# Delta rule: merges of the second and third batch of triangles moved into the attention's loop

## The chip, the cores and the metric

The kernel runs on one core of one Trainium2 chip. The core has TensorE (PE), VectorE (DVE), ScalarE (ACT), GpSimd (POOL) and SyncE (SP, which here only issues transfers), an on-chip memory of 128 partitions (SBUF), a small accumulator memory of 8 banks for matmul results (PSUM), and 16 DMA engines to and from DRAM. Each engine runs its own queue in order. The metric is device time of one launch in microseconds (us), the median of several runs.

## The reference

Two layers of a diffusion backbone work on 256 context tokens and 512 latent tokens of width 1024. A layer normalises and modulates its input, projects it once with `w_in`, and runs two groups of heads beside each other: softmax attention, and a gated delta rule in both directions. Their outputs are joined by `w_out`, and a mixture of experts follows. The delta rule is the part that matters here. It is computed in chunks of 64 tokens, and each chunk needs the inverse of a unit lower triangle:

```
lower = where(strict, einsum("bhnid,bhnjd->bhnij", kb, kc) * decay, 0)
tmat  = triangular_solve(lower + eye, eye, lower, unit_diagonal)   # 64 x 64, per head, chunk and direction
u, w  = tmat @ (vc * bc), tmat @ (kb * exp(gcum))

def step(state, xs):                     # 12 chunks, one after the other
    v_new = u_i - w_i @ state
    o_i   = qd_i @ state + a_i @ v_new
    state = state * exp(gl_i) + kd_i^T @ v_new
```

In the last layer only the latent tokens' output is needed.

## The kernel before

**Stages of a layer.** The input is normalised and projected (line 236 holds nearly all of these matmuls); within the projections the delta rule's triangles are prepared. Then comes a loop in which the attention, the 12 steps of the delta rule and the modulation vectors for later stages are interleaved. The output projection, the routing and the experts follow.

**Triangles.** The 12 chunks lie in six token tiles of two chunks. `PAIRS` makes three batches of them: tiles 0 and 1, tiles 2 and 5, tiles 3 and 4. Step s of the loop takes chunk s forwards and one chunk backwards, so steps 0 to 3 need batch 0, steps 4 and 5 batch 1, steps 6 and 7 batch 2, and so on. A 64 x 64 triangle is inverted in two halves. `delta_intra` (called by `intra_batch`) makes the triangles; it keeps the off-diagonal 32 x 32 blocks in SBUF tiles `uo` (line 799) and writes the diagonal blocks to DRAM (`db`). `delta_subst` loads these (`sB`), inverts them by 31 steps of two DVE instructions each (lines 821 and 822), one after the other, and writes the result to DRAM (`dy`). `delta_merge` loads the inverted blocks in another layout (`yl`, line 834, four transfers), transposes them on DVE (line 835), makes two masked copies for each direction on ACT (`xm`, line 840), multiplies by the off-diagonal blocks in two groups of 128 small matmuls (lines 848 and 852) with an eviction between them (line 849), adds the product on DVE (line 856), and stores the full inverse to DRAM (`xad`, line 857). `xm` has one buffer, so the copies for the second direction reuse it after the first direction's store has landed. The two products stand in one PSUM tile of two banks (`psS`), of which there is only one; the attention's scores (line 601) use the same.

**Order before the loop.** `ORDER` lists, for each layer, the projections and the delta rule's pieces in program order: `c` is a convolved projection, `n` a plain one, `i` is `intra_batch`, `s` is `delta_subst`, `m` is `delta_merge`, `x` the query products. All three merges stand near the end, `m2` last.

**The loop.** `kv_stacks` loads keys and values once projections are done (their tiles take over the place of the projections' inputs) and splits the keys into two parts, `ka` and `kb` (lines 569 to 575). `attn_queries` loads and splits queries (`ql`, lines 583 to 591). `attn_slots` runs the attention in units of one head and 128 queries, `ada_steps` the modulation: four weight loads of 1 MB and matmuls for a chunk of 1024, an accumulator `ac` (lines 264 and 266) and a store of it (line 280). `step_load` fetches a step's `lk`, `lx` and `lq` (lines 867 to 873). `PAT` interleaves the three by letters: `d` is the step, `f` the attention, `a` the modulation.

**What sets the order of work.** Nothing is pinned in these stages: `pin` acts only inside the experts. A planner goes through all instructions with its own estimate of durations, and takes among those that are ready the earliest in program order. So `ORDER` and `PAT` are priorities, and the result is one fixed order for each engine and each queue. A tile with all its buffers in use makes its next writer wait for the last reader.

Of the kernel before, what the change touches and what calls it, by code (L numbers as in the profile page):

```python
# [13 lines left out]
F32 = mybir.dt.float32  # L14
# [3 lines left out]
AF = mybir.ActivationFunctionType  # L18
# [23 lines left out]
def const_table():  # L42
# [4 lines left out]
    def put(name, a):  # L47
# [56 lines left out]
UO = 6  # L104
# [18 lines left out]
ORDER = ("c4 c5 c6 c7 S i0 s0 i1 s1 i2 s2 c0 c1 c2 c3 Q n256 n0 x n512 m0 m1 c8 c10 c11 c9 n2304 m2",  # L123
         "c4 c5 c6 c7 S c0 i0 s0 i1 s1 c9 i2 s2 c1 c2 c3 Q n256 n0 x n512 m0 m1 c8 c10 n2304 c11 m2")
# [17 lines left out]
class Model:  # L142
# [125 lines left out]
    def ada_steps(self, i, ch, pool, q):  # L268

        nc = self.nc  # L270
        eng = getattr(nc, q)
        acc = pool.tile([P, UNIT], F32, tag="ac", bufs=2, name="ac")
        ab = pool.tile([P, UNIT], F32, tag="ab", bufs=1, name="ab")
        eng.dma_start(ab, self.t["ada_b"][i, ch * D:(ch + 1) * D].rearrange("(g o j) -> g o j", g=4, o=1).to_broadcast([4, 32, UNIT]))
        for n in range(4):
            self.ada_part(i, ch, n, acc, lambda w, g: w[:, g * UNIT:(g + 1) * UNIT], pool, 2, q)
            if n < 3:
                yield
        nc.vector.tensor_tensor(acc, acc, ab, op=OP.add)
        eng.dma_start(self.md[i][ch], acc)  # L280
        yield
# [296 lines left out]
    def attn_queries(self, qd, pr, q0, nq, pool):  # L578

        nc, pin = self.nc, self.pin  # L580
        n = nq * P
        x = pool.tile([P, 4, P], F32, tag="ql", bufs=2, name="ql")
        self.q("att").dma_start(x[:, :nq], qd[:, q0:q0 + nq, pr * P:(pr + 1) * P])
        ps = self.psA("qt")
        for q in range(nq):
            pin(nc.tensor.transpose(ps[:, q * P:(q + 1) * P], x[:, q, :], self.ident))
        qs = pool.tile([P, 2, 512], F32R, tag="qs", bufs=2, name="qs")
        for e in range(2):
            o, r = 64 * e, 64 * (1 - e)
            pin(nc.scalar.activation(qs[o:o + 64, e, :n], ps[o:o + 64, :n], AF.Copy))  # L590
            pin(nc.vector.tensor_tensor(qs[r:r + 64, e, :n], ps[o:o + 64, :n], qs[o:o + 64, e, :n], op=OP.subtract))
        return qs
# [232 lines left out]
    def delta_merge(self, tts, dy, us, xad, pool):  # L825


        nc = self.nc
# [6 lines left out]
        nc.vector.transpose(yt, yl)  # L835
        xb, xt = (yt[:, 0], yl[:, 1]), (yl[:, 0], yt[:, 1])
        x = [pool.tile([P, 2, NH, HD], F32, tag="xm", bufs=1, name="xm") for d in range(2)]
        for d in range(2):
            for q in range(2):
                nc.scalar.activation(x[d][:, :, :, 32 * q:32 * q + 32], xb[d], AF.Copy, scale=self.C["quad"][:, q:q + 1])  # L840
        g = pool.tile([P, 512], F32, tag="mg", bufs=1, name="mg")
        ps = self.psS("mg")
        pa, pb = ps[:, :512], ps[:, 512:]
        place = [(d, 32 * (2 * c2 + d), 32 * (2 * c2 + 1 - d)) for d in range(2) for c2 in range(2)]
        blocks = [(t, h, slice((t * NH + h) * 32, (t * NH + h + 1) * 32)) for t in range(2) for h in range(NH)]
        for t, h, c in blocks:
            for d, ra, rb in place:
                nc.tensor.matmul(pa[rb:rb + 32, c], us[tts[t]][ra:ra + 32, h, :], xt[d][ra:ra + 32, t, h, :], start=True, stop=True, tile_position=(ra, rb))
        nc.scalar.activation(g, pa, AF.Copy, scale=-1.0)
        for t, h, c in blocks:  # L850
            for d, ra, rb in place:
                nc.tensor.matmul(pb[ra:ra + 32, c], g[rb:rb + 32, c], xb[d][rb:rb + 32, t, h, :], start=True, stop=True, tile_position=(rb, ra))
        a, b = tts
        for d in range(2):
            y = x[d][:, :, :, 32 - 32 * d:64 - 32 * d]
            nc.vector.scalar_tensor_tensor(y, pb.rearrange("p (t h i) -> p t h i", t=2, h=NH), self.C["quad"][:, d:d + 1], y, op0=OP.mult, op1=OP.add)
            self.q("ix").dma_start(xad[a:b + 1:b - a, d, :, 0].rearrange("t p f -> p t f"), x[d].rearrange("p t h i -> p t (h i)"))

    def step_load(self, s, vk, xad, qkd, need, pool):
# [9 lines left out]
        if need:  # L869
            a = pool.tile([P, 512], F32, tag="lq", bufs=2, name="lq")  # L870
            for d in range(2):
                self.q("step").dma_start(a[rows[d]], qkd[tl[d], rows[d]])
            nc.gpsimd.tensor_tensor(x[:, 1], x[:, 1], a, op=OP.mult)
# [7 lines left out]
    def delta_step(self, s, S, kx, dT, sc, o, seen, need, pool):  # L881
# [22 lines left out]
        if s > 0:  # L904
# [5 lines left out]
            t = pool.tile([P, 512], F32, tag="yt2", bufs=1, name="yt2")  # L910
# [85 lines left out]
    def intra_batch(self, b, us, dT, sc, xad, db, pool):  # L996
# [3 lines left out]
        for d in range(2):  # L1000
            for j, tt in enumerate(PAIRS[b]):
                n = 4 * (2 * d + j)
                self.delta_intra(tt, d, kk[j], sc, us[tt], xad, db[:, n:n + 4], pool)

# [497 lines left out]
    def layer(self, i, xsrc, rows, done, xstack, mod):  # L1502
# [12 lines left out]
        dy = [dr("dy%d_" % b, [NH, 16, 32, 32]) for b in range(3)]  # L1515
        qd, gd, atd = dr("qd", [P, NT, 768]), dr("gd", [P, NT, 512]), dr("atd", [P, 4, NT * P])
# [6 lines left out]
        with self.pool("hp", B) as hp:  # L1523
            with self.pool("pj", B) as wp:
# [47 lines left out]
                with self.pool("pp", B) as pool, self.pool("q1", A) as p1:  # L1572
# [7 lines left out]
                    for op in ORDER[i].split():  # L1580
# [10 lines left out]
                        elif kind == "i":  # L1591
                            self.intra_batch(int(arg), us, dT, sc, xad, db[int(arg)], p1)
                        elif kind == "s":
                            self.delta_subst(int(arg), db[int(arg)], dy[int(arg)], p1)
                        elif kind == "m":
                            self.delta_merge(PAIRS[int(arg)], dy[int(arg)], us, xad, p1)
# [8 lines left out]
        with self.pool("at", B) as pool:  # L1605
# [9 lines left out]
            with self.pool("q2", A) as p2:  # L1615
# [4 lines left out]
                for s in range(12):  # L1620
                    nkx = load(s + 1)
                    step = self.delta_step(s, S, kx, dT, sc, o, seen, need(D0[s] // 2), p2)
                    for c in PAT[i][s % 3]:
# [145 lines left out]
```

## Time and profile before

| | us |
|---|---|
| median of 3 runs | 2127.5 |
| lowest and highest | 2121.08 and 2129.52 |
| profiled execution | 2123.24 |
| its span | 2121.4 |

| engine | busy us | share of the span |
|---|---|---|
| PE | 1758.6 | 83% |
| DVE | 1272.5 | 60% |
| ACT | 882.0 | 42% |
| POOL | 839.4 | 40% |

The profile is one execution, recorded on the chip. Times are counted from its start. Busy shares are means over stages with different limits, so they are read by stretch. "PEclk" or "granted clock" is the share of full speed that TensorE got: 1.00 is 2.4 GHz and 0.50 is 1.2 GHz. The DMA share is the mean busy share of the 16 DMA engines. PEld is TensorE's loading of weights, which overlaps its matmuls. An `x` before a number is a count of instructions, and L835 is line 835. A row's square bracket holds the idle time of that engine just before it, and what ended it.

### The profile page before, as it was taken

To read this page: it belongs to the slowest core of one execution; us is meant where nothing else is said; L and a number is where in the kernel's file an instruction comes from. 1 tells how busy PE (TensorE), PEld (TensorE's weight loads), DVE (VectorE), ACT (ScalarE), POOL (GpSimd) and SP (SyncE) were. 2 spreads that over 40 slices of the span, in tenths; PEclk is the share of its full clock that TensorE was granted. 3 is DMA by queue.
4 is the path that set the end of the run, shared out by engine and by line. 5 is a ranking of instruction groups with operands and counts; after the bars stand their busy time and mean duration, and the time that the engine had idled before them with its cause. 6 is when DMAs were issued, how large, how long until landed. Compare 5 with 4: busy or idle time off the path is not lost. (4 is left out here: it accounts for less than half of the span.)

```text
span 2121.4 us, 34943 instructions
## 1 busy us (share of the span) xinstructions
PE 1758.6 (83%) x13579; PEld 1287.2 (61%) x13579; DVE 1272.5 (60%) x2350; ACT 882.0 (42%) x1513; POOL 839.4 (40%) x915
## 2 busy tenths in 40 slices
PE   6998785678887869999996987844897769999995
PEld 4886775456666745565555876733576555566553
DVE  3468995467672445655555579984677453444443
ACT  3454333446561124444444544423565223444442
POOL 4455663253254323324225467640334632233221
PEclk9998897779997989999997998976999779999997
DMA  8223445986627398889854323365972668887872
GB/s 279 72 70 90 117 137 144 260 250 204 195 56 171 103 359 315 328 319 324 327 180 122 92 73 110 93 182 148 311 204 71 177 266 311 328 312 303 313 262 85
DMA packets 227684, 427.76 MB, mean 202 GB/s; under 512 B 83721, under 2 KB 157181, under 8 KB 202940
## 3 DMA queue, kind: packets, MB, share of 16 engines
q1 hardware_dynamic: 171547, 329.09, 46.1%
q0 software_dynamic: 33536, 72.59, 12.1%
q10 hardware_dynamic: 22432, 23.81, 3.3%
q8 instruction: 109, 1.79, 0.4%
q14 instruction: 60, 0.48, 0.1%
HBM read 386.82 MB, written 84.67 MB: 222 GB/s over the span
## 5 line engine op out<-in xcount | busy, mean ns | idle before, releaser
L1351 PE MATMUL pab<-w,xt 128*128 128x512 f32 x1024 | 465.0, 597 | 0.5 <-ACT xt L1345 0.5
L1351 PEld LDWEIGHTS pab<-w,xt 128*128 128x128 f32 x1024 | 189.3, 192 | 191.2 <-issue 186.3
L1405 POOL DMA_INDIRECT yd<-ey,idx x64 | 118.8, 1856 | 469.8 <-DMA yd<-ey,idx 196.1
L1372 DVE TENSOR_TENSOR gl<-gt,gh 128x256 fp32r<-128x256 f32 x64 | 27.2, 425 | 276.9 <-ACT gh L1371 265.2
L1330 DVE TENSOR_TENSOR w2l<-w,w2h 128x2048 fp32r<-128x2048 f32 x64 | 147.3, 2301 | 43.5 <-ACT w2h L1329 40.8
L1371 ACT ACTIVATE gh<-gt 128x256 fp32r<-128x256 f32 x64 | 24.6, 385 | 349.1 <-PE gt L1367 349.1
L486 POOL TENSOR_TENSOR wlo<-wraw,whi 128x1024 fp32r<-128x1024 f32 (+1 forms) x44 | 111.1, 2530 | 83.5 <-ACT whi L485 83.5
L236 PE MATMUL pn<-whi,hh 128*128 128x256 f32 (+1 forms) x432 | 134.5, 314 | 8.7 <-ACT gev L1541 4.7
L236 PE MATMUL pn<-wlo,hh 128*128 128x256 f32 (+1 forms) x432 | 134.2, 312 | 4.6 <-POOL wlo L486 4.6
L236 PE MATMUL po<-woh,m 128*128 128x512 f32 x320 | 114.4, 434 | 28.1 <-ACT m L1040 15.7
L236 PE MATMUL pn<-whi,hl 128*128 128x256 f32 (+1 forms) x432 | 133.3, 313 | 0.7 <-DVE hl L347 0.6
L236 PE MATMUL pt<-hh,wlo 128*128 128x512 f32 (+1 forms) x352 | 124.8, 354 | 0.0
L236 PE MATMUL pt<-hl,whi 128*128 128x512 f32 (+1 forms) x352 | 123.4, 351 | 0.0
L236 PE MATMUL pt<-hh,whi 128*128 128x512 f32 (+1 forms) x352 | 122.5, 348 | 0.0
L1329 ACT ACTIVATE w2h<-w 128x2048 fp32r<-128x2048 f32 x64 | 121.7, 1902 | 0.0
L1393 PE MATMUL py<-w2h,gh 128*128 128x512 f32 x256 | 108.1, 422 | 4.4 <-DVE ey L1400 4.4
L515 DVE SCALAR_TENSOR_TENSOR dT<-xin,cw,dT 128x772 f32<-128x772 f32 x64 | 82.7, 1295 | 43.9 <-ACT dT L513 42.2
L1345 ACT ACTIVATE xt<-xt 128x512 f32<-128x512 f32 x128 | 69.8, 596 | 85.4 <-PE xt L1344 85.3
L1393 PE MATMUL py<-w2l,gh 128*128 128x512 f32 x256 | 102.1, 399 | 0.0
L1393 PE MATMUL py<-w2h,gl 128*128 128x512 f32 x256 | 101.5, 396 | 0.0
L610 ACT ACTIVATE pp<-sc,mx 128x768 f32<-128x768 f32 (+1 forms) x80 | 65.3, 816 | 83.5 <-DVE mx L605 83.2
L236 PEld LDWEIGHTS pn<-whi,hh 128*128 128x128 f32 x432 | 90.8, 211 | 13.5 <-ACT gev L1541 4.9
(391 smaller groups left out, 4443.9 us busy)
## 6 DMA issues: line engine op xcount, KB each, us to landing
w<-w SPq DMA_DIRECT2D x192, 1024.0 KB, 9.2
araw<-ada_w POOLq DMA_DIRECT2D x40, 1024.0 KB, 9.7
wraw<-w_in SPq DMA_DIRECT2D x40, 512.0 KB, 4.3
lk<-vk SPq DMA_DIRECT2D x48, 256.0 KB, 7.2
lx<-xad SPq DMA_DIRECT2D x40, 256.0 KB, 6.9
araw<-ada_w SPq DMA_DIRECT2D x8, 1024.0 KB, 10.6
wr<-w_out SPq DMA_DIRECT2D x8, 1024.0 KB, 5.1
vk<-vr ACTq DMA_DIRECT2D x16, 384.0 KB
```

The lines of the kernel that those rows point to most:

```text
L236: self.nc.tensor.matmul(ps, a(k), b(k), start=(first and n == 0), stop=(last and n == 3 * nk - 1))
L486: getattr(nc, eng).tensor_tensor(lo, raw, hi, op=OP.subtract)
L515: nc.vector.scalar_tensor_tensor(dst, xin[:, tap:tap + 772], cw[:, tap, f:f + 1], dst, op0=OP.mult, op1=OP.add)
L610: self.pin(self.nc.scalar.activation(u.p[:, :u.nk * P], u.ps[:, :u.nk * P], AF.Exp, bias=u.mx, accum_out=u.sm))
L1329: self.pin(nc.scalar.activation(hi, src, AF.Copy))
L1330: self.pin(eng.tensor_tensor(lo, src, hi, op=OP.subtract))
L1345: pin(nc.scalar.activation(xt[:, 4 * q:4 * q + 4, :], ps.rearrange("p (k n) -> p k n", k=4), AF.Copy))
L1351: self.pin(self.nc.tensor.matmul(pa.rearrange("p (a f) -> p a f", a=2), xt[:, k, :], w13[:, :, k, :], start=(k == 0), stop=(k == 7)))
L1371: pin(nc.scalar.activation(gh, p3, AF.Copy))
L1372: pin(nc.vector.tensor_tensor(gl, p3, gh, op=OP.subtract))
L1393: pin(self.nc.tensor.matmul(py[:, n * 512:(n + 1) * 512], a[:, j, :], b[:, c], start=(j + m == 0), stop=(j == 1 and m == 2)))
L1405: self.pin(self.nc.gpsimd.indirect_dma_start(out=yd, out_offset=bass.IndirectOffsetOnAxis(ap=idx, axis=0), in_=y, in_offset=None, bounds_c ...
```

## The change

The merges of batches 1 and 2 leave `ORDER`. `delta_merge` becomes a generator of five pieces. In the loop, batch 1's pieces are called in step 0 and batch 2's in step 2, at the letters number 0, 6, 9, 13 and 17 of that step's pattern. As nothing is pinned, these are places in program order. The `uo` tiles of batches 1 and 2 no longer live until then: `intra_batch` stores them to DRAM (`ud`), and the merge loads them back. The two products of a merge stand in two narrow PSUM tiles (`psC`, one bank each). The masked copies come after the first product. To make room for the merge's tiles beside the loop's, several tiles lose a buffer: `uo` 6 to 4, `ac` 2 to 1, `ql` 2 to 1, `lq` 2 to 1, and `yt2` takes a buffer of `ot`.

```diff
@@ -101,7 +101,9 @@
...
 QS = 1
-UO = 6
+UO = 4
+XM = 1
+MG, MA = {0: 1, 2: 2}, (0, 6, 9, 13, 17)
 VR = 1
...
@@ -120,8 +122,8 @@
...
 FINP = (8, 9, 10, 11)
-ORDER = ("c4 c5 c6 c7 S i0 s0 i1 s1 i2 s2 c0 c1 c2 c3 Q n256 n0 x n512 m0 m1 c8 c10 c11 c9 n2304 m2",
-         "c4 c5 c6 c7 S c0 i0 s0 i1 s1 c9 i2 s2 c1 c2 c3 Q n256 n0 x n512 m0 m1 c8 c10 n2304 c11 m2")
+ORDER = ("c4 c5 c6 c7 S i0 s0 i1 s1 i2 s2 c0 c1 c2 c3 Q n256 n0 x n512 m0 c8 c10 c11 c9 n2304",
+         "c4 c5 c6 c7 S c0 i0 s0 i1 s1 c9 i2 s2 c1 c2 c3 Q n256 n0 x n512 m0 c8 c10 n2304 c11")
 WP = 3
...
@@ -269,7 +271,7 @@
...
         eng = getattr(nc, q)
-        acc = pool.tile([P, UNIT], F32, tag="ac", bufs=2, name="ac")
+        acc = pool.tile([P, UNIT], F32, tag="ac", bufs=1, name="ac")
         ab = pool.tile([P, UNIT], F32, tag="ab", bufs=1, name="ab")
...
@@ -579,7 +581,7 @@
...
         n = nq * P
-        x = pool.tile([P, 4, P], F32, tag="ql", bufs=2, name="ql")
+        x = pool.tile([P, 4, P], F32, tag="ql", bufs=1, name="ql")
         self.q("att").dma_start(x[:, :nq], qd[:, q0:q0 + nq, pr * P:(pr + 1) * P])
...
@@ -822,39 +824,50 @@
...
         self.q("iy").dma_start(dy.rearrange("h q r c -> (h q) r c"), Y)
-    def delta_merge(self, tts, dy, us, xad, pool):
-        nc = self.nc
+    def delta_merge(self, tts, dy, us, ud, xad, pool):
+        nc, pin = self.nc, self.pin
         yt = pool.tile([P, 2, 2, NH, 32], F32, tag="yt", bufs=1, name="yt")
...
                 self.q("ild").dma_start(yl[:, d, t], dy[:, n:n + 4].rearrange("h q r c -> (q r) h c"))
-        nc.vector.transpose(yt, yl)
+        if us is None:
+            us = {}
+            for j, tt in enumerate(tts):
+                us[tt] = pool.tile([P, NH, 32], F32, tag="ul%d" % j, bufs=1, name="ul")
+                self.q("ild").dma_start(us[tt], ud[j])
+        yield
+        pin(nc.vector.transpose(yt, yl))
         xb, xt = (yt[:, 0], yl[:, 1]), (yl[:, 0], yt[:, 1])
-        x = [pool.tile([P, 2, NH, HD], F32, tag="xm", bufs=1, name="xm") for d in range(2)]
-        for d in range(2):
-            for q in range(2):
-                nc.scalar.activation(x[d][:, :, :, 32 * q:32 * q + 32], xb[d], AF.Copy, scale=self.C["quad"][:, q:q + 1])
+        yield
         g = pool.tile([P, 512], F32, tag="mg", bufs=1, name="mg")
-        ps = self.psS("mg")
-        pa, pb = ps[:, :512], ps[:, 512:]
+        pa = self.psC("mga")
         place = [(d, 32 * (2 * c2 + d), 32 * (2 * c2 + 1 - d)) for d in range(2) for c2 in range(2)]
...
             for d, ra, rb in place:
-                nc.tensor.matmul(pa[rb:rb + 32, c], us[tts[t]][ra:ra + 32, h, :], xt[d][ra:ra + 32, t, h, :], start=True, stop=True, tile_position=(ra, rb))
-        nc.scalar.activation(g, pa, AF.Copy, scale=-1.0)
+                pin(nc.tensor.matmul(pa[rb:rb + 32, c], us[tts[t]][ra:ra + 32, h, :], xt[d][ra:ra + 32, t, h, :], start=True, stop=True, tile_position=(ra, rb)))
+        pin(nc.scalar.activation(g, pa, AF.Copy, scale=-1.0))
+        x = []
+        for d in range(2):
+            x.append(pool.tile([P, 2, NH, HD], F32, tag="xm", bufs=XM, name="xm"))
+            for q in range(2):
+                pin(nc.scalar.activation(x[d][:, :, :, 32 * q:32 * q + 32], xb[d], AF.Copy, scale=self.C["quad"][:, q:q + 1]))
+        yield
+        pb = self.psC("mgb")
         for t, h, c in blocks:
             for d, ra, rb in place:
-                nc.tensor.matmul(pb[ra:ra + 32, c], g[rb:rb + 32, c], xb[d][rb:rb + 32, t, h, :], start=True, stop=True, tile_position=(rb, ra))
+                pin(nc.tensor.matmul(pb[ra:ra + 32, c], g[rb:rb + 32, c], xb[d][rb:rb + 32, t, h, :], start=True, stop=True, tile_position=(rb, ra)))
+        yield
         a, b = tts
...
             y = x[d][:, :, :, 32 - 32 * d:64 - 32 * d]
-            nc.vector.scalar_tensor_tensor(y, pb.rearrange("p (t h i) -> p t h i", t=2, h=NH), self.C["quad"][:, d:d + 1], y, op0=OP.mult, op1=OP.add)
+            pin(nc.vector.scalar_tensor_tensor(y, pb.rearrange("p (t h i) -> p t h i", t=2, h=NH), self.C["quad"][:, d:d + 1], y, op0=OP.mult, op1=OP.add))
             self.q("ix").dma_start(xad[a:b + 1:b - a, d, :, 0].rearrange("t p f -> p t f"), x[d].rearrange("p t h i -> p t (h i)"))
+        yield
     def step_load(self, s, vk, xad, qkd, need, pool):
@@ -867,7 +880,7 @@
...
         if need:
-            a = pool.tile([P, 512], F32, tag="lq", bufs=2, name="lq")
+            a = pool.tile([P, 512], F32, tag="lq", bufs=1, name="lq")
             for d in range(2):
...
@@ -907,7 +920,7 @@
...
             yield
-            t = pool.tile([P, 512], F32, tag="yt2", bufs=1, name="yt2")
+            t = pool.tile([P, 512], F32, tag="ot", bufs=2, name="yt2")
             for e in range(2):
...
@@ -993,7 +1006,7 @@
...
         self.q("vk").dma_start(dst.rearrange("t p f -> p t f"), r.rearrange("p t e i -> p t (e i)"))
-    def intra_batch(self, b, us, dT, sc, xad, db, pool):
+    def intra_batch(self, b, us, ud, dT, sc, xad, db, pool):
         kk = [self.delta_kk(tt, 1, dT, pool) for tt in PAIRS[b]]
...
@@ -1001,6 +1014,9 @@
...
                 self.delta_intra(tt, d, kk[j], sc, us[tt], xad, db[:, n:n + 4], pool)
+        if b > 0:
+            for j, tt in enumerate(PAIRS[b]):
+                self.q("iud").dma_start(ud[b, j], us[tt])
     def gate(self, mp, ps, n, dst):
@@ -1513,6 +1529,7 @@
...
         dy = [dr("dy%d_" % b, [NH, 16, 32, 32]) for b in range(3)]
+        ud = dr("ud", [3, 2, P, NH, 32])
         qd, gd, atd = dr("qd", [P, NT, 768]), dr("gd", [P, NT, 512]), dr("atd", [P, 4, NT * P])
...
@@ -1589,11 +1606,12 @@
...
                         elif kind == "i":
-                            self.intra_batch(int(arg), us, dT, sc, xad, db[int(arg)], p1)
+                            self.intra_batch(int(arg), us, ud, dT, sc, xad, db[int(arg)], p1)
                         elif kind == "s":
...
                         elif kind == "m":
-                            self.delta_merge(PAIRS[int(arg)], dy[int(arg)], us, xad, p1)
+                            for _ in self.delta_merge(PAIRS[int(arg)], dy[int(arg)], us, None, xad, p1):
+                                pass
                         elif kind == "x":
...
@@ -1612,7 +1630,7 @@
...
             fill = self.attn_slots(work, st, qd, atd, pool)
-            with self.pool("q2", A) as p2:
+            with self.pool("q2", A) as p2, self.pool("mg2", A) as p3:
                 S, seen = [None], set()
...
@@ -1620,7 +1638,13 @@
...
                     step = self.delta_step(s, S, kx, dT, sc, o, seen, need(D0[s] // 2), p2)
-                    for c in PAT[i][s % 3]:
+                    for n, c in enumerate(PAT[i][s % 3]):
+                        if s in MG:
+                            if n == 0:
+                                b = MG[s]
+                                merge = self.delta_merge(PAIRS[b], dy[b], None, ud[b], xad, p3)
+                            if n in MA:
+                                next(merge)
                         next({"d": step, "f": fill, "a": ada}[c], None)
```

## Rows read from the trace of the kernel before

**Rows 1.** Stretches: length; busy us of PE, PEld, DVE, ACT, POOL; clock; DMA share; GB/s.

```profile
260.00:340.00 80.00, 69.29 (x916) 63.45 (x916) 77.48 (x155) 28.62 (x46) 41.00 (x38) 0.93 0.40 118
345.00:362.00 17.00, 0.32 (x4) 0.18 (x4) 0.13 (x1) 0.84 (x1) 7.89 (x9) 0.55 1.01 255
362.00:380.00 18.00, 6.01 (x263) 5.27 (x264) 8.01 (x17) 8.75 (x19) 0.74 (x1) 0.59 0.41 137
380.00:440.00 60.00, 43.67 (x639) 30.59 (x640) 29.95 (x82) 28.56 (x80) 21.59 (x27) 0.76 1.00 283
...
1420.00:1470.00 50.00, 13.73 (x545) 10.97 (x545) 22.21 (x48) 13.45 (x23) 3.78 (x4) 0.53 0.55 164
1470.00:1530.00 60.00, 47.87 (x678) 34.93 (x678) 38.66 (x77) 32.44 (x62) 15.84 (x19) 0.89 0.98 289
```

**Rows 2.** Timeline of PE, the projections' last matmuls: start, duration, line, operation.

```profile
343.40 0.28 PE L236 MATMUL pn<-whi,hl 128*128 128x256 f32 x1
...
1411.11 0.39 PE L236 MATMUL pt<-hh,wlo 128*128 128x512 f32 x1
```

**Rows 3.** Line 601, scores: first matmuls in two stretches; what ended its waits.

```profile
L601 PE MATMUL sc<-ka,qs x1: 553/553/553, 377.9 to 377.9; 128*128 128x256 f32 x1
...
L601 PE MATMUL sc<-ka,qs x4: 415/590/793, 1469.9 to 1474.6; 128*128 128x512 f32 x2, 128*128 128x256 f32 x2
...
  DVE xm L856: 14.6, 2
```

**Rows 4.** Keys: POOL's timeline, then DMA issues of both troughs (last number: us to landing).

```profile
345.87 0.84 POOL L563 DMA_DIRECT2D xl<-qd  x1
...
1413.68 0.87 POOL L563 DMA_DIRECT2D xl<-qd  x1
...
xl<-qd POOLq DMA_DIRECT2D x1, 384.0 KB, 6.6
...
xl<-qd POOLq DMA_DIRECT2D x1, 384.0 KB, 5.2
```

**Rows 5.** Line 569, key transposes of the first layer: ns, first and last start.

```profile
L569 PE MATMUL kt<-cst,xl x6: 421/421/474, 365.5 to 366.6; 128*128 128x128 f32 x6
```

**Rows 6.** Timeline of DVE in both troughs.

```profile
362.34 1.25 DVE L835 STREAM_TRANSPOSE yt<-yl 128x1024 f32<-128x1024 f32 x1 [17.21 <-DMA cr<-conv_w]
...
372.10 0.42 DVE L575 CAST kb<-kb 64x512 fp32r<-64x512 f32 x1
...
1432.36 1.25 DVE L835 STREAM_TRANSPOSE yt<-yl 128x1024 f32<-128x1024 f32 x1 [7.03 <-DMA yl<-dy]
...
1439.95 0.42 DVE L575 CAST kb<-kb 64x512 fp32r<-64x512 f32 x1
```

**Rows 7.** A merge: lines 835, 840, 856 (ns min/median/max); stretches for lines 848, 852.

```profile
L835 DVE STREAM_TRANSPOSE yt<-yl x6: 1235/1245/1246, 281.5 to 1458.1; 128x1024 f32<-128x1024 f32 x6
...
L840 ACT ACTIVATE xm<-yt,cst x12: 704/714/724, 282.8 to 1460.1; 128x512 f32<-128x512 f32 x12
...
L856 DVE SCALAR_TENSOR_TENSOR xm<-mg,cst,xm x12: 737/748/752, 302.4 to 1469.0; 128x512 f32<-128x512 f32 x12
...
282.00:285.00 3.00, 1.25 (x124) 1.14 (x124) 1.00 0.03 9
...
289.00:291.00 2.00, 1.29 (x128) 1.18 (x128) 1.00 0.04 9
```

**Rows 8.** Waits of ACT: in total, times, longest.

```profile
ACT xm L840 <- DMA xad<-xm: 25.9, 5, 7.6
```

**Rows 9.** Modulation: timelines of ACT and POOL; landing of line 280's stores (min/median/max).

```profile
417.06 0.38 ACT L264 ACTIVATE ac<-aps 128x256 f32<-128x256 f32 x1 [4.71 <-PE aps L262]
...
424.24 0.60 POOL L280 DMA_DIRECT2D md<-ac  x1
...
DMA to landing us min/median/max: 6.2/8.4/10.7
```

**Rows 10.** Line 867, a step's load `lk`, whole run.

```profile
DMA to landing us min/median/max: 4.1/7.2/24.7
```


## The prediction

> **What bounds the kernel now.** I read the page's 40 slices first: in each layer TensorE (PE) has one trough between the projections and the attention, with its clock near half. The table of stretches says why [rows 1]. From 260 to 340 us VectorE (DVE) is busy 77.5 of 80 us: the end of the projections is DVE's. From 345 to 362 PE does 0.3 us, DVE 0.1, and the DMA engines are full; from 362 to 380 nobody is full. The second layer repeats it from 1420 to 1470, longer, PE 13.7 of 50. After each trough the attention's loop starts with DMA saturated for about 60 us (1.00 and 0.98), and only then is PE the limit.
>
> Then I read PE's own times. The last projection matmul starts at 343.4 and 1411.1 [rows 2], the first score matmul at 377.9 and 1469.9 [rows 3]: troughs of 34 and 59 us. The scores were released by the merge's last DVE operation (L856, 14.6 us in the two places [rows 3]): the merge holds the only wide PSUM tile, which a score needs too. The attention itself could go sooner: the keys are issued at 345.87 and 1413.68 and land 6.6 and 5.2 us later, at 352.4 and 1418.9 [rows 4]. DVE's timeline shows what sits in front: the transpose of the triangles (L835) blocks its in-order queue to 362.3 in the first layer after 17.2 idle us, and 7.0 us in the second, until the small loads of `yl` land [rows 6].
>
> **The change part by part.**
>
> *Earlier start.* Batches 1 and 2 leave the trough; no merge stands between projections and scores, and merges take narrow PSUM tiles. What then comes last is the key chain: from the first key transpose on PE (365.5 [rows 5]) to the last key part on DVE (372.1 + 0.4 [rows 6]) is 7.0 us. First layer: 352.4 + 7.0 = 359.4 for 377.9, a gain of 18.5. Second layer: 1418.9 + 7.0 = 1425.9 at best; DVE still shares its time there with batch 2's substitution and the last convolution, as it does up to 1440 now [rows 6], so I add 6: 1432 for 1469.9, a gain of 38. Together 56; bounds 19 (the planner still puts a transpose ahead of the key chain: first layer nothing, second only one merge's 19 us) and 62.
>
> *Merges inside the loop.* Four of them (two a layer) go from places where engines idled into a loop whose PE is the limit after its first part. Per merge: PE 1.25 + 1.29 = 2.54 us, DVE 1.24 + 2 x 0.75 = 2.7, ACT 4 x 0.71 = 2.9 and one eviction [rows 7]. DVE and ACT have room in the loop (30.0 and 28.6 of 60 [rows 1]); PE's 4 x 2.5 = 10 us I count in full; below, nothing, if it falls into DMA waits. The first layer's batch 1 leaves the DVE-bound stretch 260:340, which returns 2.7.
>
> *Waits added on ACT.* `xm` keeps one buffer, so a merge's second pair of copies waits until the first half has landed in `xad`. Now ACT idles 25.9 us in five such waits, 5.2 each [rows 8], where it had little else. In the loop, exponentials and evictions of the attention are queued behind that copy, and PE waits for them. Four waits: 0 to 4 x 5.2 = 21; the planner leaves part of the time, and PE has other work for some of it: I take half, 10.
>
> `ac` falls from two buffers to one: the first eviction of a modulation chunk (L264, on ACT) now waits for the store of the chunk before. At the first change of chunk L264 runs at 417.1, the store is issued at 424.2 because POOL is blocked, and it takes 8.4 us to land [rows 9]: up to 15.6 us of wait. Eight changes in all; for the other seven I assume up to 3 each, 36 in sum. ACT is half idle there and the first falls into a stretch where PE waits for loads anyway: a third, 12; bounds 0 and 36.
>
> *DMA.* A merge moves 4 x 128 KB of `yl`, 2 x 512 KB of `xad` and now 2 x 128 KB of off-diagonal blocks back: 1.79 MB, at the loop's 283 GB/s [rows 1] 6.3 us. Two merges a layer enter the saturated part, 12.6 us. The trough leaves unused 18 x 0.59 = 10.6 us in the first layer and 50 x 0.45 = 22 in the second [rows 1], which earlier step loads and weights can fill. Bounds 0 and 25; I take 8, since prefetch is held back by two buffers. The writes of the blocks lie far ahead of their readers, in a stretch with DMA at 0.40: nothing, with SP's issues about 0.4 us each.
>
> *Smaller buffers.* `ql` with one buffer: only the first layer's short work items are at risk, 0 to 8, I take 2. `lq` with one: its reader is POOL's product directly behind the load, nothing (0 to 3). `yt2` shares two buffers with `ot`: nothing. `uo` with four: batch 2's off-diagonal copies now wait until batch 0's merge has read its own, so batch 2's substitution starts later, by up to 20 us in the second layer. Its result is wanted only in step 2 of the loop, and DVE has convolutions to do meanwhile: nothing, up to 15 if the convolutions run dry. Fewer substitution steps before the projections end could also bring those forward by up to 5.
>
> *Sum.* -56 + 10 - 3 + 10 + 12 + 8 + 2 = -17. The profiled execution took 2123.2 us (span 2121.4 and 1.8 around it), so 2106; the median of the three runs is 2127.5, 4.3 higher, so 2110. I take 2108.
>
> **The rivals.**
>
> *DMA bound, no change.* If the first 60 us of the loop simply take what the DMA engines need, an earlier start gains only DMA time that was unused: 10.6 - 12.6, so nothing, in the first layer; 22 - 12.6 = 9 in the second, and the PE term of 10 takes that back: about 2127. For it: share 1.00 and 0.98, and a step load `lk` that took 24.7 us to land [rows 10]. Against it: in those 60 us PE does 44 and 48 us, so they aren't load-bound throughout. A rule of the Trainium skill points this way: its page "DMA: Bandwidth & Descriptors", section "Issuing engines are not separate DMA queues", says that transfers from all issuing engines interleave on the same 16 DMA engines, so moving the merge's loads beside the weight stream would delay both. By that rule the time is this rival's 2127; the trace agrees that loads land late beside that stream (24.7 against 4.1 us at least [rows 10]), not that PE always waits for them.
>
> *Slower: ACT held by the copy behind `xad`.* The place is L840's second pair, the price its landing. Without that term the sum is -27 against the profile; each of the four waits counts fully if it comes while PE has nothing that doesn't need ACT. From 6.7 us each the gain is gone. If `xad`'s stores queue behind step and weight loads and take as long as a store of POOL does there at worst (10.7 [rows 9]), four make 43 and the time is 2127.5 - 27 + 43 = 2143. For it: 5.2 already without competition; against: the planner has a store's time in its plan.
>
> *The change doesn't take effect.* The order on each engine comes from a planner that believes loads to be quick. It may put batch 1's transpose before the key chain on DVE, which then waits for `yl` as now: gain 19 instead of 56. With half the engine and wait terms of a layer's trough spared, about 2127.5 - 19 + 5 - 3 + 5 + 12 + 8 = 2135.
>
> *More than expected.* If the loads of weights and steps move into the old trough and the waits hide, only the PE term is left: 2127 - 56 + 7 = 2078.
>
> **How the numbers follow.** Forecast 0.52, more than expected 0.08, DMA bound 0.17, no effect 0.08, ACT held 0.15. The forecast's own range is 2085 to 2122. Half a per cent, 10.6 us, is about what a measurement here can tell from no change: faster is under 2117, slower over 2138. Of the forecast 0.49 lies under 2117 and 0.03 within; with 0.08 that is 0.57 faster. DMA bound gives 0.02 faster, 0.13 same, 0.02 slower; no effect 0.05 same, 0.03 slower; ACT held 0.15 slower. Faster 0.59, same 0.21, slower 0.20. The range leaves out one in ten at each side: 2072 to 2145.
>
> **What would show it.** Right: first scores about 359 and 1430, troughs of 16 and 20 us; no merge operation on DVE before them; the merge's matmuls between scores; the loop's length from first to last score up by 10 to 20 us a layer. Wrong: ACT waits for `xad` or for `md`'s store over 7 us each; DVE's transposes idle for `yl` before or in the loop; the step loads landing later than now; batch 2's substitution ending after step 2 has begun. If the first scores come no earlier than 370 and 1450, the first step of the sum has failed.

## The result and the profile after

The changed kernel takes 2147.2 us (median of four runs, 2139.7 to 2153.9) against 2124.8 for the kernel before in the same comparison: ratio 1.010, 95% interval 1.006 to 1.014. It is slower; 2108 was forecast, and 2147.2 lies just outside the range. Its profiled span is 2146.6 us.

The start of the attention came earlier, as predicted; the loop then took longer than that had gained. Stretches of the changed kernel, columns as in [rows 1]:

```profile
345.00:362.00 17.00, 2.73 (x10) 2.07 (x10) 4.67 (x11) 5.48 (x11) 6.09 (x7) 0.55 1.02 340
362.00:380.00 18.00, 14.21 (x76) 10.24 (x76) 9.28 (x28) 11.90 (x35) 2.55 (x3) 0.57 1.00 242
380.00:440.00 60.00, 35.08 (x814) 25.06 (x817) 21.68 (x51) 19.87 (x51) 16.58 (x21) 0.71 0.72 200
1444.00:1470.00 26.00, 19.82 (x129) 14.89 (x133) 18.73 (x38) 16.52 (x30) 2.56 (x2) 0.57 0.81 199
1470.00:1530.00 60.00, 44.01 (x945) 32.16 (x931) 25.79 (x48) 22.20 (x41) 11.43 (x14) 0.77 0.79 242
```

From 362 to 380 PE does 14.2 us where it did 6.0. But from 380 to 440, where it did 43.7 [rows 1], it does 35.1, and DVE, ACT and the DMA engines fall too, and the granted clock, a mean over the stretch, is 0.71 for 0.76: nobody is full, so everybody waits. The second layer's 1470 to 1530 repeats it, DVE 25.8 for 38.7.

The lines that answer to [rows 2, 3, 5], and the chain of the loop's twelve delta steps, whose first matmul group is `pz`; first the scores, key transposes and `pz` of the changed kernel (counts, ns, first and last start), one row for each layer:

```profile
L603 PE MATMUL sc<-ka,qs x80: 277/476/796, 361.0 to 622.1; 128*128 128x256 f32 x48, 128*128 128x512 f32 x32
...
L603 PE MATMUL sc<-ka,qs x64: 277/415/797, 1444.0 to 1639.1; 128*128 128x512 f32 x32, 128*128 128x256 f32 x32
...
L571 PE MATMUL kt<-cst,xl x6: 421/421/447, 354.5 to 355.6; 128*128 128x128 f32 x6
...
L933 PE MATMUL pz<-lk,lx x384: 218/218/366, 372.4 to 620.2; 64*64 64x64 f32 x192
...
L933 PE MATMUL pz<-lk,lx x384: 217/218/367, 1464.2 to 1660.4; 64*64 64x64 f32 x192
```

and `pz` of the kernel before:

```profile
L920 PE MATMUL pz<-lk,lx x384: 218/218/366, 383.7 to 613.9; 64*64 64x64 f32 x192
...
L920 PE MATMUL pz<-lk,lx x384: 218/218/367, 1476.5 to 1636.8; 64*64 64x64 f32 x192
```

First scores: 361.0 for 377.9, 1444.0 for 1469.9. But the steps' chain, 230 and 160 us long before, is 248 and 196 long: it starts 11 and 12 us earlier and ends 6 and 24 later. Part of the second layer's shift comes from the first: the second layer's projections start at 1155.3 for 1145.6 us, and counted from there its chain starts 22 earlier and ends 14 later. From first to last score the loop takes 261 and 195 us for 235 and 154, where the prediction allowed 10 to 20 more. In the first layer scores and steps end together; in the second the steps end last, 13 us after the last score before and 21 after.

What stands in the chain's way first is on SP (start, duration of the issues). The output weights, 3 MB, which nobody needs until the loop's end, are issued at 342 us, ahead of the first steps' loads, of which the first goes at 349.9 and the second at 362.1; before, they went at 390, behind them. First the issues of the changed kernel, then that of the weights before, then SP's waits for the weights' transfers in the changed kernel (us in total, times, longest):

```profile
342.44 3.76 SPq L1077 DMA_DIRECT2D wr<-w_out  x3
...
349.89 0.51 SPq L880 DMA_DIRECT2D lk<-vk  x1
...
362.14 0.45 SPq L880 DMA_DIRECT2D lk<-vk  x1
```

```profile
389.54 1.61 SPq L1061 DMA_DIRECT2D wr<-w_out  x3
```

```profile
SPq L880 <- DMA wr<-w_out: 6.0, 2, 5.6
SPq L881 <- DMA wr<-w_out: 5.6, 1, 5.6
```

Then the waits that I had called signs of failure, in brackets the idle time of ACT or DVE and what ended it, all in the changed kernel:

```profile
437.35 0.38 ACT L266 ACTIVATE ac<-aps 128x256 f32<-128x256 f32 x1 [8.48 <-DMA md<-ac]
...
1502.66 1.25 DVE L843 STREAM_TRANSPOSE yt<-yl 128x1024 f32<-128x1024 f32 x1 [5.15 <-DMA yl<-dy]
...
1503.95 1.33 ACT L858 ACTIVATE xm<-yt,cst 128x512 f32<-128x512 f32 x2 [6.06 <-DVE yt L843]
...
1528.51 1.33 ACT L858 ACTIVATE xm<-yl,cst 128x512 f32<-128x512 f32 x2 [11.68 <-DMA xad<-xm]
```

and the total that L858 waits for `xad` in the two loops (us, times), the term for which I took 10:

```profile
  DMA xad<-xm: 17.4, 2
```

Four explanations were open: A, these waits; B, the smaller buffers; C, the weights ahead of the steps' loads; D, the merges' instructions between the stages of the delta steps; later H, the merges' loads. The kernel before ran at 2123.8 to 2126.6 (medians) beside the experiments; each ratio is to it, with the 95% interval in brackets. A difference between two variants is one of medians, and by these intervals it is good to some 6 to 9 us (an estimate).

### The profile page after: what moved, and what is told of

The parts are those of the page before. It is cut to its first block, busy times and chain, and to the rows that moved or that the text cites. A ratio compares the mean times of both kernels' runs of the same rounds, so it can differ in the third digit from the quotient of the medians.

```text
span 2146.6 us, 35019 instructions
## 1 busy us (share of the span) xinstructions
PE 1787.3 (83%) x13579; PEld 1311.0 (61%) x13579; DVE 1281.4 (60%) x2350; ACT 880.7 (41%) x1513; POOL 842.2 (39%) x915
## 5 line engine op out<-in xcount | busy, mean ns | idle before, releaser
L1360 PEld LDWEIGHTS xt<-cst,xe 128*128 128x128 f32 x512 | 67.9, 192 | 49.4 <-issue 29.8
```

The costliest lines, as they stand in the source:

```text
L1360: pin(nc.tensor.transpose(ps[:, k * P:(k + 1) * P], xe.rearrange("p (q k) -> p k q", k=8)[:, 4 * q + k, :], self.ident))
```

## Experiments

**B: buffers.** e1, the kernel before with the cuts alone:

```diff
-UO = 6
+UO = 4
-tag="ac", bufs=2 ; tag="ql", bufs=2 ; tag="lq", bufs=2 ; tag="yt2", bufs=1
+tag="ac", bufs=1 ; tag="ql", bufs=1 ; tag="lq", bufs=1 ; tag="ot", bufs=2
```

> The kernel before, merges where they were, with only the smaller buffers of the change (uo 4 for 6, ac, ql and lq 1 for 2, the yt2 tile taken from ot's two). Theory A (the merges' own waits, in order on ACT and DVE, stop TensorE): the buffers cost little, 2125 to 2131. Theory B (the smaller buffers cost the time: the loop after waits up to 8.5 us for md's store at ac and 12.8 us for ql's transposes): 2138 to 2155.

Measured 2151.2, ratio 1.0127 (1.010 to 1.015). Without the move the cuts cost 26 us, but part of it before the loop (last projection 352.3 for 343.4, third substitution stored at 355 for 343), so not all of it can be the changed kernel's, whose projections and third substitution end at 343.1 and 342 as before. e2, the changed kernel with the buffers back:

```diff
-UO = 4 ; ac, ql, lq bufs=1
+UO = 6 ; ac, ql, lq bufs=2
-g = pool.tile([P, 512], F32, tag="mg", ...)
+g = ul.rearrange("p t h i -> p (t h i)")
```

> The changed kernel with the buffers of before restored (uo 6, ac, ql, lq 2; the merge's evicted product takes the place of the off-diagonal blocks it was made from, so that there is room). Theory B: the loss goes and the earlier start stays, 2095 to 2115. Theory A: 2140 to 2150, unless ac's wait is part of it (8.5 us in the first layer, 7.8 in the second): then 2132.

Measured 2154.8, ratio 1.0134 (1.010 to 1.017): no gain, but this does not yet refute B, because the sum hides a second thing: the planner made a new order, and in it DVE has a scaling of the tail (`s`) ahead of the second layer's last step and idles 16.3 us for its load. In the first layer, which that does not touch, the buffers gained nothing either: the second layer starts at 1159.1 for 1155.3. PE's timeline in e2:

```profile
1685.74 2.04 PE L935 MATMUL pz<-lk,lx 64*64 64x64 f32 x32 [19.63 <-DVE lk L928]
```

**A: the copies' wait for `xad`.** e3, in the changed kernel:

```diff
-x[1] = pool.tile(..., tag="xm", bufs=XM)   # waits until x[0] is stored
+x[1] = [yl[:, 0], yt[:, 1]]                # dead after the first matmul group
```

> The changed kernel with the second half of the inverse built in the two halves of yl and yt that are dead by then, so that ACT's second pair of copies no longer waits for xad's store to land (5.7 us in the first layer, 11.7 us in the second in the changed kernel's trace); six small ACT and DVE operations more per merge. Theory A: most of 17 us comes back, 2130 to 2136. Theory B: nothing, 2143 to 2150. Theory C (step loads late behind the output weights on the queues): nothing, 2143 to 2150.

Measured 2162.6, ratio 1.017 (1.014 to 1.020). The same new order spoils it: the last step idle 18.8 us. Inconclusive by itself.

**C: the weights.** e4, the changed kernel with one order on SP:

```diff
+self.sl = (last DMA of step_load)
 r = nc.sync.dma_start(raw, w_out...)
+add_manual_dep(r, self.sl)   # order on the queue, no wait
```

> The changed kernel with the output weights' three 1 MB loads held on SP behind the loads of step 5 and later, as their place in the program is; now they go at 342 us and 1466 us, ahead of the first steps' loads. Theory C: the first steps' loads and yl land up to 9 us earlier (3 MB at 340 GB/s) in the first layer, 2130 to 2138. Theories A and B: 2143 to 2150; a little less if yl is what the transposes wait for.

Measured 2132.7, ratio 1.0036 (1.0015 to 1.0057): 14.5 us back, C's prediction. The first layer's scores now end at 604.8, before 612.7, and the first steps' loads go at 349 and 350. Nearly all of the gain is in the first layer: the second starts at 1135.9 for 1155.3, and its `pz` run from 1443.7 to 1639.8, 196 us as in the changed kernel. e8, the same order in the kernel before:

```diff
 (kernel before)
+add_manual_dep(r, self.sl)
```

> The kernel before with the output weights held back on SP as in the other version: they went at 390 and 1484 us, behind the loads of the first three steps. If holding them back helps only because the change had let them go ahead of the first steps' loads (342 and 1466 us): 2121 to 2129. If it helps any kernel whose loop starts with full DMA engines: 2108 to 2118.

Measured 2122.3, ratio 0.999 (0.997 to 1.001): nothing. So the 14.5 us belong to the change, which let the weights go early; whether freed memory did that, or only the new order, was not tried.

**A again,** where the trace of e4 shows it at its largest; ACT's copies and PE, start, duration, and the idle time ahead:

```profile
1481.85 1.33 ACT L858 ACTIVATE xm<-yt,cst 128x512 f32<-128x512 f32 x2 [10.94 <-DVE yt L843]
...
1511.81 1.33 ACT L858 ACTIVATE xm<-yl,cst 128x512 f32<-128x512 f32 x2 [19.18 <-DMA xad<-xm]
...
1484.06 1.54 PE L625 MATMUL ptr<-cst,pp 128*128 128x128 f32 x6 [9.88 <-ACT pp L617]
...
1514.45 0.79 PE L603 MATMUL sc<-ka,qs 128*128 128x512 f32 x1 [9.95 <-ACT pp L612]
```

PE stands 20 us behind ACT's two waits. e5 takes both out:

```diff
+tag="yl", bufs=2 in the loop      # loads before the first merge is done
+x[1] = [yl[:, 0], yt[:, 1]]       # as e3, on e4
```

> The version with the output weights held back, and both waits of a merge taken out: two buffers for yl in the loop, so that batch 2's loads go before batch 1 is done, and the inverse's second half in dead halves of yl and yt, so that ACT's copies don't wait for xad (room for it: the evicted product lies where the off-diagonal blocks lay). In the version with held-back weights TensorE stood 9.9 us in the second layer while DVE's transposes waited for yl, and 10.0 us while ACT's copies waited for xad. Theory A (these waits are what is left of the loss): 2105 to 2118. Theory D (the merges' instructions, in order between the stages of delta steps 0 to 3, delay the recurrence, which sets the loop's end, waits or not): 2127 to 2137.

Measured 2130.8, ratio 1.001 (0.999 to 1.004), D's range. ACT's two waits are gone from the trace, the `yl` loads of both merges are issued by 1459 us, and the time stays: the second layer's `pz` still run from 1447.4 to 1644.6, 197 us. The edit is not pure: it adds six small operations and two stores to each merge, and DVE's next transpose now waits until the half that lies in `yt` is stored, 6.0 us in the first layer, 3.0 in the second:

```profile
DVE yt L845 <- DMA xad<-yt: 3.0, 1, 3.0
```

So A's waits on ACT do not explain the sum; what a merge without any wait would cost, e5 does not show.

**D: place.** e9, on e4, the matmul groups behind the step's `su` and new state:

```diff
-MA = (0, 6, 9, 13, 17)
+MA = ((0, 6, 15, 20, 24), (0, 6, 14, 16, 17))
```

> The version with the output weights held back, merges still in steps 0 and 2, but their two matmul groups given places behind the step's own state product su and its new state S, instead of ahead of them; all the rest as it was. In that version su of the second layer's step 0 ran at 1456.5 us though its operand was there at 1448.0, with both merge groups between. Theory D (the merge's place between the stages of a delta step delays the recurrence): steps 0 to 4 of the second layer take 65 to 72 us instead of 85, time 2112 to 2124. Theory A (only the waits for yl and xad count, which stay): 2127 to 2138.

Measured 2129.7, ratio 1.002 (1.000 to 1.004): A's range. The second layer's steps 0 to 4 (first `pz` of the first step to first `pz` of the fifth) took 80 us for 85 in e4, not 65 to 72, so D in this form falls too. e6, on e4, later steps:

```diff
-MG = {0: 1, 2: 2}
+MG = {2: 1, 4: 2}
```

> The version with the output weights held back, and the merges in steps 2 and 4 of the loop instead of 0 and 2, still ahead of the steps that load their results. Theory A: the waits move with the merges but the DMA is less full by then (0.71 to 0.85), so half of 20 us comes back: 2118 to 2128. Theory D: the merges stand between the stages of steps 2 to 4 instead of 0 to 2, nothing gained: 2128 to 2138. Theory E (what costs is that the merges come while the first steps' loads are late): 2100 to 2115.

Measured 2119.1, ratio 0.996 (0.994 to 0.998): 13.6 us come back, as A had it, though e5 spoke against A's waits as the price. e11 joins the two:

```diff
+MG = {2: 1, 4: 2}, MA = ((0, 6, 16, 20, 24), (0, 6, 14, 16, 17))
```

> Merges in steps 2 and 4, their matmul groups behind su and S, output weights held back: the two edits that theories D and E ask for together. Theory D: 2106 to 2115. If the place within a step does not count: 2115 to 2123, as with the merges in steps 2 and 4 alone.

Measured 2131.6, ratio 1.003 (1.001 to 1.005): worse than e6, against both expectations. So the place within a step has no fixed sign. e7, what an earlier first score alone is worth, in the kernel before:

```diff
-ps = self.psS("mg"); pa, pb = ps[:, :512], ps[:, 512:]
+pa = self.psC("mga") ... pb = self.psC("mgb")
```

> The kernel before with one edit: the merges take two narrow PSUM tiles instead of the wide one, so no merge holds the tile that the first score needs; nothing is moved. Theory F (the loop's end is set by the chain of twelve delta steps, which starts at 384 and 1476 us whatever the scores do): 2119 to 2130. The prediction's first step (an earlier first score is time gained): 2105 to 2117.

Measured 2135.9, ratio 1.0036 (1.001 to 1.006). First scores come at 361.9 and 1450.5, 16.0 and, from the layer's start, 14.0 us earlier, and nothing is gained. Not clean: the merges now hold narrow tiles that the projections use, which end at 350.7 for 343.4, and in the second layer 30 us later counted from its start. The traced execution took 2124.9, 11 less than the median.

**What the merges cost at all.** e10, on e4, none in the loop:

```diff
-next(merge) at MA: loads, transposes, matmuls, copies, stores
+nc.vector.memset(xz, 0.0); two stores of xz into xad
```

> The version with the output weights held back, with the merges' work left out of the loop: in steps 0 and 2 two stores of zeros into xad stand for all of it, so the inverses of batches 1 and 2 are not computed (no loads of triangles, transposes, matmuls, copies). What is left is the early start and the loop. Theory D with F (the delta steps set the loop's end, and the merges slow them): steps 0 to 4 take 53 to 60 us in the second layer, 2080 to 2098. If the loads of the first steps are what slows the loop's start, merges or not: 2108 to 2125.

Measured 2095.7, ratio 0.986 (0.982 to 0.989). Against e4 the merges cost 37 us in the loop. What is left, the early start with the smaller buffers, is worth 29.5. `pz` of e10:

```profile
L933 PE MATMUL pz<-lk,lx x384: 218/218/366, 365.6 to 595.0; 64*64 64x64 f32 x192
...
L933 PE MATMUL pz<-lk,lx x384: 218/218/366, 1435.8 to 1607.0; 64*64 64x64 f32 x192
```

The first layer's chain is as long as before, 229 us, and simply 18 earlier; the second's is 171 for the 196 of e4. That difference lies in the steps beside which the merges stand: steps 0 to 4 take 57 us, as D with F expected, for 85 in e4, and the rest 114 for 111. e13 puts back the loads alone, e14 the instructions alone, e15 the instructions without ACT's wait for `xad`:

```diff
 e13: e10
+dma_start(yl[:, d, j], dy...) x4, dma_start(ul, ud...) x2, no reader
 e14: e4
-dma_start(yl...), dma_start(ul...)
+nc.gpsimd.memset(yl, 0.0), memset(ul, 0.0)
 e15: e14
+x[1] = [yl[:, 0], yt[:, 1]]
```

> As the version without merges (2095.7 us), with the merges' loads put back: in steps 0 and 2 yl and the off-diagonal blocks are loaded, 4 + 2 loads each, and nothing reads them (the inverses of batches 1 and 2 are not computed). Theory H (the loads themselves cost, in the full DMA engines, by delaying the steps' loads and the weights): 2108 to 2120 of the 37 us between 2095.7 and 2132.7. Theory A or D (waits or work): 2094 to 2101.

> The version with held-back weights and merges in steps 0 and 2, whose triangles and off-diagonal blocks are set to zero by POOL instead of loaded (the inverses of batches 1 and 2 are then not the right ones): every other instruction of a merge stays, the wait of ACT's second copies for xad too. Theory A, its yl half (DVE's transposes wait for yl): 2115 to 2122. Theory D (the instructions themselves, in order between the steps' stages): 2127 to 2135.

> As the one before (triangles set to zero by POOL, not loaded), and the inverse's second half built in dead halves of yl and yt, so that ACT's second copies wait for nothing: a merge's instructions without any wait for a DMA. Theory A: 2096 to 2108, only the instructions' own 2.5 us on TensorE per merge over the version without merges. Theory D: 2122 to 2135.

Measured 2118.0, ratio 0.996 (0.994 to 0.998), 2123.4, ratio 0.997 (0.995 to 1.000), and 2130.2, ratio 1.001 (0.999 to 1.003). Loads alone cost 22.3 us, instructions alone 27.7, together 37: both, and they overlap. Taking the wait for `xad` away gained nothing a third time. But e14 and e15 bring a wait of their own: POOL, which also issues queries and modulation weights, in order, can zero `ul` only when the matmuls on its old content are done, 15.5 us in e14's second layer (1440 to 1520). So 27.7 may be too much, and 2123.4 lies between the two expected ranges. The loads, theory H: what all DMA queues moved from 1436 to 1493 us, with the engines full in both (share 1.02 and 1.05), in e10, then in e13:

```profile
DMA packets 6187, 17.44 MB, mean 306 GB/s; under 512 B 921, under 2 KB 921, under 8 KB 6181
```

```profile
DMA packets 13866, 15.29 MB, mean 268 GB/s; under 512 B 9061, under 2 KB 9573, under 8 KB 13860
```

`yl` comes in rows of 32 numbers, 128 bytes: 1024 pieces a load, 8192 for two merges, which is the difference in small packets (8140). They are 1 MB, and over 3 MB of other loads had to give way. In the first layer, from 345 to 434 us, it was 22.05 MB for 25.19. They also hold SP, whose queue the steps' loads share: issuing one took 1.1 us in the median in e13's first layer (ns min/median/max), 0.73 in its second:

```profile
L1652 SPq DMA_DIRECT2D yl<-dy x8: 365/1124/4650, 369.3 to 395.0; - x8
```

e17 is e13 with the same bytes in pieces of 1 KB; the small pieces move to the store:

```diff
-dy = dr("dy", [NH, 16, 32, 32])
+dy = dr("dy", [16, 32, NH, 32])
-dma_start(dy, Y)
+for h in range(NH): dma_start(dy[:, :, h], Y[16 * h:16 * h + 16])
```

> As the version with the merges' loads alone in the loop (2118.0), but the inverted triangles lie in DRAM so that a partition's part of yl is one piece of 1 KB instead of eight of 128 bytes; the pieces of 128 bytes are now on the side of the store of the triangles, eight issues for one, before the loop. Same bytes. Theory H1 (the loads cost by the number of their small pieces: in the 57 us from 1436 us 13866 packets moved 15.3 MB with them, 6187 packets 17.4 MB without): 2097 to 2108. Theory H2 (they cost by their bytes, or by their place on SP's queue): 2113 to 2122.

Measured 2102.7, ratio 0.988 (0.985 to 0.992): H1's range: 15.3 of the loads' 22.3 us are the price of pieces, not of bytes. In the first layer's stretch e17 moves 24.44 MB for e13's 22.05; in the second's only 15.49 for 15.29, where the small pieces of the last store run into the loop's start (4661 packets under 512 bytes). The same row in e17's first layer (median 0.43 us in its second):

```profile
L1653 SPq DMA_DIRECT2D yl<-dy x8: 319/384/1609, 366.0 to 387.2; - x8
```

**A better version.** e12, e6 with the buffers of before:

```diff
+MG = {2: 1, 4: 2}; UO = 6; ac, ql, lq bufs=2; g in ul's place; weights held back
```

> Merges in steps 2 and 4, output weights held back, and the buffers of before restored (uo 6; ac, ql, lq 2). Theory B (the smaller buffers cost some of the loop's time): 2105 to 2114. Otherwise 2115 to 2123. If the order at the loop's end changes as in the changed kernel with restored buffers (last two delta steps of the second layer behind the tail's first loads): 2145 to 2165.

Measured 2114.3, ratio 0.995 (0.993 to 0.997): faster than both kernels. It is 4.7 under e6, between B's range and the other and within what these differences can tell, so a price of the buffers is not shown. In its trace, of an execution of 2103.9, 10 under the median, `pz` end at 602.1 and 1617.7. e16, e12 with batch 1 back among the projections, and e18, e12 with e17's layout:

```diff
 e16:
+MG = {4: 2}, m1 in ORDER
 e18:
+dy = dr("dy", [16, 32, NH, 32])
```

> Output weights held back, the buffers of before, only batch 2's merge in the loop (step 4), batch 1's back among the projections: one merge fewer per layer in the loop, one more in front of it. If each merge in the loop costs a share of the 37 us and one more among the projections costs nothing before the loop: 2103 to 2112. If the second merge in the trough brings back the wait of the key chain behind the transposes on DVE: 2113 to 2122.

> The best full version so far (merges in steps 2 and 4, output weights held back, buffers of before: 2114.3) with the same layout of the triangles in DRAM. Theory H1: 2098 to 2110. Theory H2: 2111 to 2119. If the eight stores for one delay SP's queue before the loop, or the planner's order at the loop's end turns: over 2120.

Measured 2143.5, ratio 1.007 (1.004 to 1.010), and 2131.0, ratio 1.003 (1.000 to 1.005). e16 lies above both its ranges, e18 in its last, over 2120. In e16 a second merge in narrow tiles stands among the projections, as in e7, and probably in their way: they end at 349.8 for 338.5 in e12, and in the second layer 21 us later counted from its first `pt` matmul. In e18 the first layer's scores end at 616.6 for 600.0 and PE once waits 12.5 us for queries; why the new order is that bad is not settled.

## Why the prediction was wrong

*The earlier start* was right as a time and wrong as a gain, and this is the step that failed: "Together 56". The first score was to come at 359 and came at 361.0; in the second layer 38 us were to be won from the layer's start and 35.6 were (1469.9 - 1145.6 = 324.3 before, 1444.0 - 1155.3 = 288.7 after). (In the first layer [rows 6] name `cr`, a small load issued behind `yl`, as what DVE waited for, not `yl`; that changed nothing.) I counted every microsecond of that as time, as if the loop behind it kept its length. But scores share the loop with the chain of twelve delta steps, which ends last in the second layer, and I never asked when its first step could start. In e10, with no merge in its way, first scores come 24 and 35 us earlier (from the layer's start: 1420.4 - 1130.9 = 289.5), first steps 18 and 26, last scores 16 and 24, last steps 19 and 15; the time is 29.5 lower. Most of what is missing is in the second layer: the first hands over 14.7 us earlier, for 18.5 forecast, and the second wins 15 for 38. e10 also has the smaller buffers and no batch 1 among the projections, so of the sum it should be held against -56 - 3 + 14 = -45. Why the second layer's steps keep so little, and what the buffers have in it, was not isolated.

*Merges in the loop* were priced at 10 for PE, 10 for `xad` and 8 for DMA: 28. They cost 37. PE's 2.5 us each were fair [rows 7]; the loads were not. I worked them out from bytes at the loop's 283 GB/s; alone they cost 22.3 us, inside my bounds of 0 and 25 but near the wrong end, and 15 of that is the size of their pieces. The Trainium skill, page "DMA: Bandwidth & Descriptors", section "Specifications", gives 512 bytes as the least transfer that runs at line rate. e17 agrees: 7.0 us for the loads in pieces of 1 KB where pieces of 128 bytes cost 22.3. What the instructions add beyond their busy time, up to 27.7 us alone for four merges, is not settled to a place: neither the waits on ACT (e5, e15) nor the order behind `su` (e9) accounts for it, only a later step helps (e6). A part may be that each edit gives a new planned order. A part may be TensorE's clock, which no run isolates: from 355 to 434 us PE is busy 59.9 us in e14 and 60.0 in e10, at a granted clock of 0.66 and 0.85.

*What was not in the sum:* the weights ahead of the steps' loads, 14.5. I had seen that earlier loads would fill the trough, and counted it as help; the planner filled it with the transfer that is needed last.

*Waits on ACT.* They are there: 17.4 for `xad`, 0 to 21 were my bounds. The rival "ACT held by the copy behind `xad`" came nearest to the number, 2143 for 2147.2, but by luck: three experiments without that wait (e3, e5, e15) gained nothing, each with six small operations more a merge, e3 with a spoiled order. "DMA bound" was right that moved transfers cost the loop, but priced them by bytes, at 2127, and not right that an early start beside full DMA engines is worth nothing (e10). `yl` in the loop stopped DVE's queue for 5.2 us once in the second layer, which I had at nothing.

*Small buffers.* `ac` waits 8.5 us at the first change of chunk, within the 15.6 that I had bounded, and 21.2 in four waits in all, where I took 12 and bounded 36; of the 14 us for `ac` and `ql` e12 against e6 shows 4.7, with intervals that overlap. `uo` at nothing was right: the second layer's projections end 247.8 us after its first `pt` matmul with six buffers (e12), 248.5 with four (the changed kernel). Both are 10 later than before (238.6), where I had hoped for 5 earlier; why was not tried.

The three differences, e10 against the kernel before, e4 against e10 and the changed kernel against e4, add up to the 22 us by construction, so their sum proves nothing. What they give is shares of the miss: the start -29.5 for -45, the merges 37 for 28, the weights 14.5 for nothing, 15.5 + 9 + 14.5 = 39, which is the way from -17 to +22. The start is the largest, but with errors of 6 to 9 us each the order of the three is open.

## What to carry to other kernels

An earlier first instruction is not by itself a gain: find the chain of the stage's last instruction, and ask when its first link can start. Price a load by its pieces as well as its bytes, above all where it is moved from an idle stretch into one with full DMA engines, and ask which prefetch the new order will let go ahead of it. Where a planner makes the order, one edit moves everything: read each variant stage by stage, and trust a cause only when putting a thing in and taking it out agree.

## What the runs showed of the hardware

Rows of 128 bytes cost twice. With the DMA engines full for 57 us, 13866 packets moved 15.3 MB (e13) where 6187 had moved 17.4 MB (e10). And in the loop SP was held for issuing one load of 1024 pieces 1.1 and 0.73 us in the median (e13's two layers), from 0.37 to 5.15, against 0.38 and 0.43 with pieces of 1 KB (e17). The same bytes in longer pieces made the whole kernel 15.3 us faster, though the small pieces only moved to a store ahead of the loop.
